# Four-row reads of the first part of each expert's down matrix, in a hybrid diffusion backbone on one Trainium2 core

## The chip, the core and the metric

The kernel runs on one core of one Trainium2 chip, in float32. A core has a matrix engine (PE, with its weight loads shown apart as PEld), a vector engine (DVE), a scalar engine (ACT), GpSimd (POOL), a synchronisation engine (SP) that here issues nearly all reads from device memory, and 16 DMA engines that move the data. The metric is device time of one launch in microseconds (us), the median of the runs; less is better. One MiB is 1.0486 MB.

## The reference

Two layers work on 256 latent tokens and 256 context tokens of width 1024. The first layer (attention beside a convolution, then a dense SwiGLU) and the mixer of the second (a state-space scan in two directions) are the same in both kernels. The change touches the last stage, the second layer's mixture of experts:

```python
logits = (hf @ w_router).astype(jnp.float32)
top_v, top_i = lax.top_k(logits, TOP_K)              # 2 of 8 experts for each of 256 tokens
top_w = jax.nn.softmax(top_v, axis=-1)
...
for e in range(N_EXPERTS):                           # w1, w3: 1024 x 3584, w2: 3584 x 1024
    out = out + gates[:, e:e + 1].astype(hf.dtype) * swiglu(hf, w1[e], w3[e], w2[e])
```

`swiglu(h, w1, w3, w2)` is `(silu(h @ w1) * (h @ w3)) @ w2`. The three matrices of one expert are 42 MiB, those of all eight 336 MiB (352 MB), and each is read once.

## The kernel before

A tile framework takes the Python program, schedules it with a timing model of its own, and writes one fixed queue of instructions for each engine. Each queue is worked off in order: an instruction that waits for a semaphore holds up all that stand behind it on its engine.

**The expert stage.** Eight experts are worked one after the other; here they are called expert 0 to 7 in that order. Only the tokens of an expert are gathered, in groups of 32: `GROUPS = (3, 2, 3, 2, 3, 2, 3, 1)`, the larger counts in the places with three groups. The hidden width of 3584 is split in two parts by `SS`: part 0 has 2048 columns (four blocks of 512, one for each quarter of PE's columns), part 1 has 1536 (four of 384). An expert's reads, in the order of its units, are:

- `up(0)`: 8 reads of w1 and 8 of w3, 128 x 2048, 1 MiB each (8 KB for each of the 128 partitions);
- `up(1)`: 8 of w1 and 8 of w3, 128 x 1536, 0.75 MiB each (6 KB for each partition);
- `down(0)`: 8 reads of w2, 1 MiB each: 256 rows, two adjacent rows (8 KB) to a partition;
- `down(1)`: 4 reads of the same kind, and 2 of 1 MiB in which each partition gets two single rows of 4 KB.

`turn(s)` transposes the hidden activations so that they fit the rows of `down(s)`; the transposes take every second column, because a partition holds two adjacent rows. `gather(e + 1)` fetches the next expert's tokens between `up(1)` and `down(0)`; `scatter` of an expert runs inside the next one. `slot_map` reads one small tile (`prow`) for each expert.

**Reads and slots.** `run` walks over the pieces of all experts and loads up to `AHEAD = 20` pieces ahead of the one that PE multiplies. Every read takes the next slot of a ring of 21 slots of 8 KB for each partition (`rings`, filled from the pools `rawe`, `t8`, `rawp`, `hlp` and `rawm`). A read is issued on SP (line 148, in `load`) and can't be issued before PE has finished with the slot's last content. Each read also carries one of eight completion semaphores in turn (`DMAHW0` to `DMAHW7` below), and waits for the read eight before it: no more than eight are under way.

In PE's queue the up matmuls are on line 1533, the down matmuls on line 1598, the gather on line 1486, the transposes on line 1566, the scatter on line 1622.

Of the kernel before, what the change touches and what calls it, by code (L numbers as in the profile page):

```python
# [10 lines left out]
F32 = mybir.dt.float32  # L11
# [8 lines left out]
P = 128  # L20
D = 1024
# [69 lines left out]
class Net:  # L91
# [44 lines left out]
    def load(self, view, pool=None):  # L136

        if isinstance(view, View):
            view = view.get()
        pieces = view if isinstance(view, list) else [(slice(0, P), view)]  # L140
        kk, n = pieces[0][1].shape[1:]
        if pool == "t8":
            t = self.wk([P, 2048], "t8")
        else:
            t = (pool or self.rawp).tile([P, 2048], F32, tag="hl" if pool is self.hlp else "raw", name=self.nm("raw"))
        v = t[:, :kk * n].rearrange("p (k n) -> p k n", k=kk)
        for sl, src in pieces:
            self.nc.sync.dma_start(v[sl], src)
        return v
# [17 lines left out]
    def run(self, units, ahead=2, pools=None):  # L167

        pieces = []
        for u in units:  # L170
            if u.views is None:
                pieces.append((u, None, 0, 0, 0, True, True))
                continue
            for vi, view in enumerate(u.views):
                kk, n = (view[0][1] if isinstance(view, list) else view).shape[1:]
                kp = max(1, self.SPLIT // n) if u.split else kk
                base = sum((w[0][1] if isinstance(w, list) else w).shape[1] for w in u.views[:vi])
                for k0 in range(0, kk, kp):
                    m = min(kp, kk - k0)
                    pieces.append((u, vi, k0, m, base, vi == 0 and k0 == 0,  # L180
                                   vi == len(u.views) - 1 and k0 + m == kk))
        loaded, parts, npc, seen, held = {}, {}, {}, {}, []
        for p in pieces:
            npc[id(p[0])] = npc.get(id(p[0]), 0) + 1
            seen[id(p[0])] = 0
        nxt = 0
        for i, (u, vi, k0, m, base, first, last) in enumerate(pieces):
            nahead = sum(1 for q in range(i + 1, nxt) if pieces[q][1] is not None)
            while nxt < len(pieces) and (nxt <= i or nahead < ahead):
                pu, pv, pk, pm, pb = pieces[nxt][:5]  # L190
                if pv is not None:
                    if (id(pu), pv) not in loaded:
                        loaded[id(pu), pv] = self.load(pu.views[pv], self.ring() if self.rings else None)
                    v = loaded[id(pu), pv]
                    sc = pu.scale(pb + pk) if pu.scale else None
                    parts[nxt] = self.wparts(v, pk, pm, sc) if pu.split else (v, None)
                    nahead += nxt > i
                nxt += 1
            if first and u.begin:
                u.begin()  # L200
            if vi is not None:
                hv, lv = parts.pop(i)
                if u.blocks and npc[id(u)] - seen[id(u)] <= u.tail:
                    held += [(base + k0 + c, hv[:, c], lv[:, c]) for c in range(m)]
                    for b in u.blocks if last else ():
                        for q in held:
                            u.mm(*q, [b])
                        u.end(b)
                else:
                    for c in range(m):  # L210
                        u.mm(base + k0 + c, hv[:, c], lv[:, c] if u.split else None)
                seen[id(u)] = seen.get(id(u), 0) + 1
            if last:
                held = []
                if u.end and not u.blocks:
                    u.end()
            self.tick()
# [1301 lines left out]
    def expert(self, e, n_g):  # L1519

        nc, A = self.nc, self.A
        st = {}
# [30 lines left out]
        def turn(s):  # L1553


            n = self.SS[s][1]

            def call():
                st["hT", s] = hT = self.wk([P, n // P, 3, P], f"hT{s}", bufs=1)
                for g in range(n_g):  # L1560
                    pt = self.ps("h")
                    for c in range(n // P):
                        t = st["g"][g][:, c // 2 * 256:c // 2 * 256 + min(256, n - c // 2 * 256)]
                        if t.shape[-1] == 256:
                            t = t.rearrange("p (i j) -> p j i", j=2)[:, c % 2]
                        nc.tensor.transpose(pt[:, c * P:(c + 1) * P], t, self.ident)
                    o, i = hT[:, :n // P, g], pt[:, :n].rearrange("p (c t) -> p c t", t=P)
                    if g % 2:
                        nc.vector.tensor_copy(o, i)
                    else:  # L1570
                        nc.scalar.copy(o, i)
            return Unit(begin=call)

        def down(s):
            r0, n = 4 * self.SS[s][0] // 4, self.SS[s][1]
            rows = lambda r, m: (lambda w: w[:, r:r + m])
            pair = lambda w: w.rearrange("o (i j) n -> i (o j) n", j=2)

            pieces = []
            for p in range(4):  # L1580
                for c in range(n // 256):
                    f = rows(r0 + n * p + 256 * c, 256)
                    pieces.append((lambda w, f=f: pair(f(w)), [(p, 2 * c), (p, 2 * c + 1)]))
            if n % 256:
                for p in (0, 2):
                    f = rows(r0 + n * p, 2 * n)
                    pieces.append((lambda w, f=f: f(w).rearrange("o (s i) n -> i (o s) n", s=2)[n - P:n],
                                   [(p, n // P - 1), (p + 1, n // P - 1)]))

            def begin():  # L1590
                if s == 0:
                    st["y"] = [self.ps("y") for _ in range(0, n_g, 2)]

            def mm(k, wv, _):
                p, c = pieces[k // 2][1][k % 2]
                for g in range(n_g):
                    for q in range(4):
                        nc.tensor.matmul(st["y"][g // 2][32 * q:32 * q + 32, g % 2 * 256:g % 2 * 256 + 256],  # L1598
                                         st["hT", s][:, c, g, 32 * p:32 * p + 32], wv[:, 256 * q:256 * q + 256],
                                         start=s == 0 and k == 0 and g % 2 == 0,  # L1600
                                         stop=s == 1 and k == 4 * n // P - 1 and (g % 2 == 1 or g == n_g - 1),
                                         tile_position=(0, 32 * q))

            return Unit([self.weights("od_ex_w2", e, [P, 2, D], f) for f, _ in pieces], mm, begin,
                        evict if s else None, False)

        def evict():
# [98 lines left out]
        self.n_ring += 1  # L1706
        return self.rings[self.n_ring % len(self.rings)]

    AHEAD = 20

    def late(self):

# [117 lines left out]
def build(tc, A, out, dbg=None):  # L1830
    net = Net(tc, A, out, dbg)
# [5 lines left out]
    with ExitStack() as ctx, tc.tile_pool(name="cp", bufs=1) as net.cp, \  # L1837
# [4 lines left out]
        with tc.tile_pool(name="t8p", bufs=9) as net.t8p, ExitStack() as early:  # L1842
            net.ecp = early.enter_context(tc.tile_pool(name="ecp", bufs=1))
            with tc.tile_pool(name="xcp", bufs=1) as net.xcp, tc.tile_pool(name="rawx", bufs=1) as net.rawx, \
                    tc.tile_pool(name="wp", bufs=1) as net.wp:
                with psum("psa", g=4, c=1, t=2, o=1) as net.psp:
                    h = net.phase1()
                with psum("psb", g=6, t=2) as net.psp:
                    h = net.phase1b(*h)
            with tc.tile_pool(name="op", bufs=1) as net.op, tc.tile_pool(name="wp2", bufs=1) as net.wp, \  # L1850
                    psum("psc", g=4, y=1, t=3) as net.psp:
                net.phase2(h)
            early.close()
            with psum("psm", h=6, y=2) as net.psp, tc.tile_pool(name="mp", bufs=1) as net.mp:
                net.t_tag = "h"
                with tc.tile_pool(name="rp", bufs=1) as net.wp:
                    net.route()
                with tc.tile_pool(name="ep", bufs=1) as net.wp, tc.tile_pool(name="rawm", bufs=5) as rawm:
                    net.rings = [net.rawe] + ["t8"] * 9 + [net.rawp] * 3 + [net.hlp] * 3 + [rawm] * 5
                    net.n_ring = -1  # L1860
                    net.moe()

# [12 lines left out]
```

## Time and profile before

| | us |
|---|---|
| median of 3 runs (1911.69 to 1915.6) | 1913.47 |
| the profiled execution's own time | 1911.85 |
| its span, first to last instruction | 1910.1 |
| expert stage, first up matmul to the end of the span | 1065.2 to 1910.1 |

How to read it: the page gives the busy share of each engine in 40 slices of the span, and what the DMA engines moved in each. A line of the timeline is a run of instructions of one kind on one engine, with the idle time just before it in brackets. A table of waits sums, for one engine, the time that it stood still, by what ended that wait. For SP a wait costs nothing by itself as long as earlier reads are still moving.

### The profile page before, as it was taken

Reading aid. Unit: us, or ns where it says so; the run is one execution under the profiler, and the core shown is the slowest. Engines: PE = TensorE matmul, PEld = TensorE weight load, DVE = VectorE, ACT = ScalarE, POOL = GpSimd, SP = SyncE. Lnnn points to the kernel's source line nnn. Section 1 sums busy time; section 2 is a strip of 40 time slices with the busy share of each in tenths; the row PEclk is TensorE's granted clock in tenths of the full one; section 3 lists DMA queues with packets and bytes.
Section 4 is the critical chain, followed back from the end, with each engine's and each line's share of the span. In section 5 each row is a group of like instructions: output and inputs, shape, how many; then the busy total and the mean of one; then the engine's idle time right before and its main releaser. Section 6 shows DMA issues by size and latency. Waiting matters only on the chain. (4 is left out here: it accounts for less than half of the span.)

```text
span 1910.1 us, 33591 instructions
## 1 busy us (share of the span) xinstructions
PE 1778.9 (93%) x14384; PEld 1110.9 (58%) x14384; DVE 703.5 (37%) x1143; ACT 519.1 (27%) x969; POOL 174.1 (9%) x167
## 2 busy tenths in 40 slices
PE   6999998999999989989989999999999999899964
PEld 3675356788888868757667445445644463435411
DVE  3395546334334356798887110101110101002001
ACT  3434454231222335756874100100000000001000
POOL 0064000000000014133320000000000000000000
PEclk8999999999999999989899899999999999999976
DMA  8543765422323243323357899999999999999995
GB/s 319 178 157 120 250 184 189 135 96 89 109 89 98 81 142 103 122 84 115 101 197 279 320 399 418 416 418 416 418 416 417 417 417 412 414 419 413 417 413 230
DMA packets 131574, 497.87 MB, mean 261 GB/s; under 512 B 11312, under 2 KB 18392, under 8 KB 102744
## 3 DMA queue, kind: packets, MB, share of 16 engines
q1 hardware_dynamic: 126808, 487.25, 66.3%
q10 hardware_dynamic: 4608, 8.39, 1.3%
q8 instruction: 115, 1.88, 0.4%
q14 instruction: 43, 0.35, 0.1%
HBM read 494.45 MB, written 1.15 MB: 259 GB/s over the span
## 5 line engine op out<-in xcount | busy, mean ns | idle before, releaser
L1533 PE MATMUL h<-raw,xe 128*32 128x512 f32 (+1 forms) x2664 | 265.6, 551 | 15.8 <-DMA raw<-in_od_ex_w_dram 15.8
L244 PE MATMUL g<-t,whl 128*128 128x512 f32 (+1 forms) x608 | 237.4, 390 | 0.0
L243 PE MATMUL g<-t,whl 128*128 128x512 f32 (+1 forms) x608 | 234.8, 396 | 2.1 <-ACT opad L1057 1.9
L245 PE MATMUL g<-t,whl 128*128 128x512 f32 (+1 forms) x608 | 232.7, 390 | 0.8 <-POOL whl L164 0.8
L1533 PE MATMUL h<-t,xe 128*32 128x384 f32 (+1 forms) x2200 | 214.9, 543 | 7.7 <-DMA t<-in_od_ex_w_dram 7.7
L164 DVE TENSOR_TENSOR whl<-raw,whl 128x1024 fp32r<-128x1024 f32 x109 | 137.7, 1266 | 206.6 <-ACT whl L161 206.1
L161 ACT CAST whl<-raw 128x1024 fp32r<-128x1024 f32 x129 | 134.5, 1049 | 269.9 <-PE g L245 234.3
L1533 PEld LDWEIGHTS h<-raw,xe 128*32 128x32 f32 x2664 | 97.8, 111 | 175.2 <-issue 113.2
L1544 DVE TENSOR_TENSOR g<-g,h 128x512 f32<-128x512 f32 (+1 forms) x38 | 23.6, 621 | 425.9 <-PE h L1533 238.6
L244 PE MATMUL g<-whl,t 128*128 128x512 f32 (+1 forms) x432 | 168.0, 392 | 9.2 <-DVE whl L164 7.3
L245 PE MATMUL g<-whl,t 128*128 128x512 f32 (+1 forms) x432 | 164.4, 389 | 0.0
L243 PE MATMUL g<-whl,t 128*128 128x512 f32 (+1 forms) x432 | 160.5, 394 | 1.9 <-DVE t L641 1.8
L1533 PEld LDWEIGHTS h<-t,xe 128*32 128x32 f32 x2200 | 79.1, 110 | 136.1 <-issue 91.8
L1598 PE MATMUL y<-raw,hT 128*32 128x256 f32 x2512 | 144.7, 388 | 9.7 <-DMA raw<-in_od_ex_w_dram 9.7
L1541 ACT ACTIVATE g<-h 128x512 f32<-128x512 f32 (+1 forms) x38 | 20.7, 544 | 448.9 <-PE h L1533 448.9
L243 PEld LDWEIGHTS g<-t,whl 128*128 128x128 f32 x608 | 116.6, 192 | 29.3 <-ACT opad L1057 2.3
L244 PEld LDWEIGHTS g<-t,whl 128*128 128x128 f32 x608 | 116.3, 191 | 23.7 <-issue 1.0
L245 PEld LDWEIGHTS g<-t,whl 128*128 128x128 f32 x608 | 115.4, 190 | 24.2 <-POOL whl L164 1.0
L428 POOL TENSOR_SCALAR rsv<-sst 128x1 f32<-128x1 f32 (+1 forms) x15 | 4.7, 311 | 1295.0 <-DVE sst L421 1294.8
L1598 PEld LDWEIGHTS y<-raw,hT 128*32 128x32 f32 x2512 | 80.0, 112 | 72.4 <-DMA raw<-in_od_ex_w_dram 15.0
L1598 PE MATMUL y<-t,hT 128*32 128x256 f32 x1744 | 103.4, 395 | 10.7 <-DMA t<-in_od_ex_w_dram 10.7
L1612 DVE TENSOR_TENSOR ys<-y,g2r 128x512 f32<-128x512 f32 (+1 forms) x12 | 6.6, 577 | 260.6 <-PE y L1598 260.6
(349 smaller groups left out, 2091.1 us busy)
## 6 DMA issues: line engine op xcount, KB each, us to landing
raw<-in_od_ex_w_dram SPq DMA_DIRECT2D x138, 1024.0 KB, 18.0
t<-in_od_ex_w_dram SPq DMA_DIRECT2D x102, 1024.0 KB, 19.2
raw<-in_od_ex_w_dram SPq DMA_DIRECT2D x68, 768.0 KB, 15.0
t<-in_od_ex_w_dram SPq DMA_DIRECT2D x60, 768.0 KB, 15.8
raw<-in_ev_ff_w_dram SPq DMA_DIRECT2D x32, 1024.0 KB, 5.1
raw<-in_ev_ada_w_dram SPq DMA_DIRECT2D x24, 1024.0 KB, 6.7
raw<-in_od_ada_w_dram SPq DMA_DIRECT2D x24, 1024.0 KB, 5.2
raw<-in_od_w_in_dram SPq DMA_DIRECT2D x20, 1024.0 KB, 5.2
```

Of the source, the lines that this page charges most:

```text
L161: self.nc.scalar.copy(hv, v[:, k0:k0 + m])
L164: eng.tensor_tensor(lv, v[:, k0:k0 + m], hv.bitcast(F32), op=ALU.subtract)
L243: mm(out, l[0], r[0], start=start, stop=False)
L244: mm(out, l[0], r[1], start=False, stop=False)
L245: mm(out, l[1], r[0], start=False, stop=stop)
L428: nc.gpsimd.tensor_scalar(v[:, :m], ss, inv_n, EPS, op0=ALU.mult, op1=ALU.add)
L1533: nc.tensor.matmul(st[i][g][32 * p:32 * p + 32, :n], st["x"][:, k, 32 * g:32 * g + 32], wv[:, n * p:n * p + n], start=k == 0, stop=k == KD ...
L1541: nc.scalar.activation(st["g"][g], st[0][g][:, :n], AF.Silu)
L1544: nc.vector.tensor_mul(st["g"][g], st["g"][g], st[1][g][:, :n])
L1598: nc.tensor.matmul(st["y"][g // 2][32 * q:32 * q + 32, g % 2 * 256:g % 2 * 256 + 256], st["hT", s][:, c, g, 32 * p:32 * p + 32], wv[:, 256 ...
L1612: nc.vector.tensor_tensor(ys[:, g:g + m], st["y"][g // 2][:, :256 * m].rearrange("p (g n) -> p g n", g=m), self.g2.unsqueeze(1).to_broadca ...
```

## The change

The first part of w2, 8 reads of 1 MiB for each expert, becomes 4 reads of 2 MiB: 512 rows, four adjacent rows (16 KB) to a partition. They go to a pool of their own, `rawb`, with two slots of 16 KB for each partition. Four slots of the small ring are given up for it, so that 17 are left, and `AHEAD` falls from 20 to 18. The transposes of part 0 take every fourth column instead of every second. Number and size of all matmuls stay as they are, and so do all other reads.

```diff
-        if pool == "t8":
+        if kk * n > 2048:
+            t = self.rawb.tile([P, 4096], F32, tag="rawb", name=self.nm("rawb"))
+        elif pool == "t8":
...
-                        loaded[id(pu), pv] = self.load(pu.views[pv], self.ring() if self.rings else None)
+                        big = isinstance(pu.views[pv], View) and np.prod(pu.views[pv].shape[1:]) > 2048
+                        loaded[id(pu), pv] = self.load(pu.views[pv], self.ring() if self.rings and not big else None)
...
-                        if t.shape[-1] == 256:
+                        if s == 0:
+                            t = st["g"][g].rearrange("p (i j) -> p j i", j=4)[:, c]
+                        elif t.shape[-1] == 256:
...
-                for c in range(n // 256):
+                for c in range(n // 256 if s else 0):
...
-            if n % 256:
+            if s == 0:
+                for p in range(4):
+                    f = rows(n * p, n)
+                    pieces.append((lambda w, f=f: f(w).rearrange("o (i j) n -> i (o j) n", j=4),
+                                   [(p, c) for c in range(4)]))
+            else:
...
-    AHEAD = 20
+    AHEAD = 18
...
-                with tc.tile_pool(name="ep", bufs=1) as net.wp, tc.tile_pool(name="rawm", bufs=5) as rawm:
-                    net.rings = [net.rawe] + ["t8"] * 9 + [net.rawp] * 3 + [net.hlp] * 3 + [rawm] * 5
+                with tc.tile_pool(name="ep", bufs=1) as net.wp, tc.tile_pool(name="rawm", bufs=1) as rawm, \
+                        tc.tile_pool(name="rawb", bufs=2) as net.rawb:
+                    net.rings = [net.rawe] + ["t8"] * 9 + [net.rawp] * 3 + [net.hlp] * 3 + [rawm]
```

The framework sets the queues anew for the changed program. All that stands ahead of the expert stage keeps its order. Two places of the expert stage, first SP's queue in expert 4 (three groups), where the reads of w2 begin. In these rows a name is that of the slot's tile, and the brackets hold the semaphores for which the instruction waits: `PE` is PE's, `DVE` that of DVE, `DMAHW`n those of reads. Before:

```order
L148 DMA t8_1693_11249<-in_od_ex_w3_dram 128x1536 [waits DMAHW5_49,PE_49]
...
L148 DMA t8_1694_11263<-in_od_ex_w2_dram 128x2048 [waits DMAHW6_49,PE_49]
...
L148 DMA t8_1695_11277<-in_od_ex_w2_dram 128x2048 [waits DMAHW7_49,PE_49]
...
L148 DMA raw_1706_11369<-in_od_ex_w2_dram 128x2048 [waits DMAHW2_49,PE_49]
L1501 DMA prow_1831_12732<-posd_1367_7901 128x2x128 [waits DMAHW3_49,DVE_49]
...
L148 DMA raw_1710_11386<-in_od_ex_w2_dram 128x2048 [waits DMAHW4_49,PE_49]
```

and now:

```order
L150 DMA raw_1677_11244<-in_od_ex_w3_dram 128x1536 [waits DMAHW5_49,PE_49]
...
L150 DMA rawb_1678_11258<-in_od_ex_w2_dram 128x4096 [waits DMAHW6_49]
...
L150 DMA rawb_1679_11272<-in_od_ex_w2_dram 128x4096 [waits DMAHW7_49]
L1504 DMA prow_1805_12683<-posd_1365_7900 128x2x128 [waits DMAHW0_49,DVE_49]
...
L150 DMA rawb_1688_11336<-in_od_ex_w2_dram 128x4096 [waits DMAHW6_49,DMAHW1_49,PE_49]
...
L150 DMA rawb_1692_11353<-in_od_ex_w2_dram 128x4096 [waits DMAHW7_49,DMAHW2_49,PE_49]
...
L150 DMA raw_1693_11367<-in_od_ex_w2_dram 128x2048 [waits DMAHW3_49]
```

The third big read (`rawb_1688`) takes the slot of the first, waits for PE to be done with it, and stands in SP's queue ahead of the six reads of `down(1)` and of all reads of expert 5. Experts 1 to 7 all have this order.

The second place is SP's queue around expert 0. There the first two big reads stand before the reads of `up(1)`, with no wait for PE:

```order
L150 DMA raw_1347_7771<-in_od_ex_w1_dram 128x1536 [waits DVE_49,DMAHW0_49,PE_49,Pool_49]
L150 DMA rawb_1376_8006<-in_od_ex_w2_dram 128x4096 [waits DMAHW1_49]
L150 DMA rawb_1377_8020<-in_od_ex_w2_dram 128x4096 [waits DMAHW2_49]
L150 DMA raw_1348_7773<-in_od_ex_w1_dram 128x1536 [waits DMAHW3_49,PE_49]
...
L150 DMA raw_1387_8087<-in_od_ex_w2_dram 128x2048 [waits DMAHW5_49,PE_49]
...
L150 DMA raw_1419_8453<-in_od_ex_w1_dram 128x2048 [waits DMAHW5_49,PE_49]
L150 DMA rawb_1382_8056<-in_od_ex_w2_dram 128x4096 [waits DMAHW6_49,PE_49]
L150 DMA rawb_1386_8073<-in_od_ex_w2_dram 128x4096 [waits DMAHW7_49,PE_49]
...
L150 DMA raw_1420_8503<-in_od_ex_w3_dram 128x2048 [waits DMAHW0_49,PE_49]
```

Before, these places held six reads of `up(1)` in a row, and the reads of `down(0)` followed those of `up(1)`:

```order
L148 DMA raw_1347_7768<-in_od_ex_w1_dram 128x1536 [waits DVE_49,DMAHW0_49,PE_49,Pool_49]
L148 DMA raw_1348_7770<-in_od_ex_w1_dram 128x1536 [waits DMAHW1_49]
L148 DMA raw_1349_7772<-in_od_ex_w1_dram 128x1536 [waits DMAHW2_49]
L148 DMA raw_1350_7774<-in_od_ex_w1_dram 128x1536 [waits DMAHW3_49]
L148 DMA raw_1351_7776<-in_od_ex_w1_dram 128x1536 [waits DMAHW4_49]
L148 DMA raw_1355_7793<-in_od_ex_w1_dram 128x1536 [waits DMAHW5_49,PE_49]
...
L148 DMA raw_1376_7979<-in_od_ex_w2_dram 128x2048 [waits DMAHW3_49,PE_49]
```

Now the third and fourth big read of expert 0 stand behind its six reads of `down(1)` and the first eleven reads of expert 1 (`raw_1419` is the eleventh). From `raw_1387`, the first read of `down(1)`, to `raw_1419` there are 17 small reads, so the next, `raw_1420`, takes the slot of `raw_1387`. PE's queue follows suit: four of expert 1's up pieces stand between the second and the third big piece of expert 0.

```order
L1608 MATMUL y_1417_8354<-rawb_1377_8020,hT0_1378_8037 32x256 x4
L1536 MATMUL h_1431_8720<-t8_1396_8187,xe_1408_8306 32x512 x4
...
L1536 MATMUL h_1432_8721<-t8_1402_8232,xe_1408_8306 32x512 x4
L1608 MATMUL y_1416_8353<-rawb_1382_8056,hT0_1378_8037 32x256 x8
...
L1608 MATMUL y_1416_8353<-raw_1387_8087,hT1_1411_8335 32x256 x8
```

Before, the pieces of expert 0's `down(0)` and `down(1)` stood there in a row, with none of expert 1 among them.

## Rows read from the trace of the kernel before

**Rows 1.** The page: the span in 40 slices, 47.75 us each.

```profile
PE   6999998999999989989989999999999999899964
PEclk8999999999999999989899899999999999999976
DMA  8543765422323243323357899999999999999995
GB/s 319 178 157 120 250 184 189 135 96 89 109 89 98 81 142 103 122 84 115 101 197 279 320 399 418 416 418 416 418 416 417 417 417 412 414 419 413 417 413 230
```

**Rows 2.** Stretches: us, busy us of each engine, granted clock, DMA share, GB/s.

```profile
core 0: us, PE busy (x) PEld busy (x) DVE busy (x) ACT busy (x) POOL busy (x), PEclk, DMA share, GB/s
1150.00:1200.00 50.00, 50.00 (x772) 24.94 (x768) 1.02 (x2) 1.19 (x2) 0.00 (x0) 1.00 1.01 417
1800.00:1850.00 50.00, 35.28 (x288) 8.55 (x280) 5.01 (x12) 1.67 (x3) 0.00 (x0) 0.83 1.01 413
...
1250.00:1284.00 34.00, 34.00 (x448) 14.38 (x444) 0.69 (x1) 1.05 (x2) 0.00 (x0) 1.00 1.01 419
1287.00:1312.00 25.00, 25.00 (x252) 10.34 (x248) 6.68 (x15) 1.17 (x2) 0.00 (x0) 1.00 1.01 416
```

**Rows 3.** What SP waited for, 1140 to 1890 us: total us, times, longest.

```profile
SPq L148 <- DMA raw<-in_od_ex_w_dram: 277.9, 157, 3.4
SPq L148 <- DMA t<-in_od_ex_w_dram: 205.7, 117, 3.3
SPq L148 <- PE y L1598: 35.7, 21, 6.9
SPq L148 <- PE h L1533: 27.1, 39, 1.3
```

**Rows 4.** Reads: count, KB each, median us from issue to landing; page, then 1023 to 1033 us.

```profile
raw<-in_od_ex_w_dram SPq DMA_DIRECT2D x138, 1024.0 KB, 18.0
...
t<-in_od_ex_w_dram SPq DMA_DIRECT2D x2, 1024.0 KB, 5.1
```

**Rows 5.** PE's timeline: expert 4 begins, its down part begins; the same of expert 6.

```profile
1465.84 1.06 PE L1533 MATMUL h<-raw,xe 128*32 128x512 f32 x8 [0.63 <-DMA raw<-in_od_ex_w_dram]
...
1547.21 7.11 PE L1598 MATMUL y<-t,hT 128*32 128x256 f32 x128
...
1680.72 3.64 PE L1533 MATMUL h<-t,xe 128*32 128x512 f32 x32 [0.64 <-DMA t<-in_od_ex_w_dram]
...
1762.52 7.86 PE L1598 MATMUL y<-raw,hT 128*32 128x256 f32 x120
```

**Rows 6.** PE's timeline: expert 0's down part, expert 1 begins, its down part begins.

```profile
1146.28 28.70 PE L1598 MATMUL y<-raw,hT 128*32 128x256 f32 x528
1174.80 7.95 PE L1598 MATMUL y<-t,hT 128*32 128x256 f32 x144
1182.57 7.91 PE L1533 MATMUL h<-t,xe 128*32 128x512 f32 x72
...
1239.35 12.29 PE L1598 MATMUL y<-raw,hT 128*32 128x256 f32 x224
```

**Rows 7.** PE's timeline: up and down pieces of expert 3; expert 5 from its last up piece.

```profile
1381.18 17.35 PE L1533 MATMUL h<-raw,xe 128*32 128x512 f32 x160
...
1437.97 14.02 PE L1598 MATMUL y<-t,hT 128*32 128x256 f32 x256
...
1641.50 1.50 PE L1533 MATMUL h<-t,xe 128*32 128x384 f32 x16 [0.38 <-DMA t<-in_od_ex_w_dram]
1642.93 3.81 PE L1486 MATMUL h<-pm,h 128*128 128x96 f32 x32
1646.58 0.87 PE L1566 MATMUL h<-ka,g 128*128 128x128 f32 x6
1647.38 3.00 PE L1598 MATMUL y<-raw,hT 128*32 128x256 f32 x50
```

**Rows 8.** PE's timeline: expert 7's last down piece, after the last read has landed.

```profile
1891.29 1.93 PE L1598 MATMUL y<-raw,hT 128*32 128x256 f32 x16 [1.45 <-DMA raw<-in_od_ex_w_dram]
```

More of the change, by code (lines that the diff above doesn't have):

```diff
@@ L1594, in mm @@
             def mm(k, wv, _):
-                p, c = pieces[k // 2][1][k % 2]
+                p, c = pieces[k // 2][1][k % 2] if s else pieces[k // 4][1][k % 4]
                 for g in range(n_g):
@@ L1602, in mm @@
                                          tile_position=(0, 32 * q))
-            return Unit([self.weights("od_ex_w2", e, [P, 2, D], f) for f, _ in pieces], mm, begin,
+            return Unit([self.weights("od_ex_w2", e, [P, len(a), D], f) for f, a in pieces], mm, begin,
                         evict if s else None, False)
```

## The prediction

> **What bounds the kernel now.** I began with the page's 40 slices. From slice 25 on (about 1150 us) the DMA engines are busy 9 tenths or more and move 412 to 419 GB/s to the end of the reads, while PE is also busy nearly all the time [rows 1]. The stretches tell the two apart: the DMA share is 1.01 there and the rate 416 to 419 GB/s whatever PE does, and in the last expert, where PE has 35 of 50 us of work, the rate is still 413 [rows 2]. So the reads set the end, and PE follows. PE is not far behind being a bound: with three groups it needs longer for an expert than the reads take, with two groups less. It falls behind in the even experts and catches up in the odd ones; in expert 4 and expert 6 it begins with the first read just landed (a wait for DMA ahead of the first piece), and by the last expert it waits for single reads [rows 5, 8].
>
> Then SP, which issues the reads. Its long waits are for earlier reads (483.6 us in 274 waits), not for PE (62.8 us) [rows 3]: eight reads are always under way, and a 1 MiB read lands 18.0 us after its issue, though a lone one takes 5.1 [rows 4]. Slots have not been what reads wait for. The question for the change is whether SP ever stands still so long that those eight run out, since idle time of the DMA engines is added to the end in full.
>
> **Prices.** From the first read of expert 4 to the first of expert 6, both waited for by PE, 84 MiB arrive in 1680.72 - 1465.84 = 214.9 us [rows 5]: 2.56 us for a MiB, 5.1 for a big read. A lone read takes 5.1 - 2.5 = 2.6 us beyond its transfer [rows 4]; I take that as the time from an issue into an empty queue to new data. PE's time for a big piece is 36.3 us / 672 x 96 matmuls = 5.2 us with three groups [rows 6], 14.02 / 256 x 64 = 3.5 with two [rows 7], and half of that, 1.75, with one.
>
> **What the change removes.** 64 reads become 32, and packets of 8 KB ones of 16 KB. Reads with 8 KB packets run at 419 GB/s, those with 6 KB at 416 [rows 2]. If a packet has a fixed cost, 0.7% between 6 and 8 KB makes 1.1% between 8 and 16: of 64 MiB x 2.51 = 161 us that is 1.7 us. From below it is bounded by nothing, from above by some 6 us (the same step three times over, as reading error of 419 and 416 allows). I take 2 us, near the row. The Trainium skill's HBM Reference, section Specifications, has a core streaming alone at about 425 GB/s; by that figure these reads could gain 2.3 us, as an estimate.
>
> Nothing else gets cheaper. The 76 transposes of part 0, at 0.87 / 6 = 0.145 us [rows 7], are 11 us in all; a stride of four for two would have to slow them by a third to cost 4 us, and that would fall on PE, which mostly follows. I cost it at nothing.
>
> **What the change adds: one wait per expert.** In experts 1 to 7 SP's queue now holds the third big read right behind the first two, and it waits until PE is done with the first. Behind it in SP's queue stand all further reads, so when the second big read has landed, the DMA engines have nothing left. Their idle time is: PE's end on the first big piece, plus 2.6, less the landing of the second.
>
> *Experts 2, 4, 6 (three groups).* Let time begin when PE starts on the first up read, just landed. PE reaches the first down piece 1547.21 - 1465.84 = 81.4 us later in expert 4, and 81.8 in expert 6 [rows 5]. By then 27 more MiB of up reads and the first big read have long landed: 29 x 2.56 = 74.2; the second at 79.3. PE ends the first big piece at 81.4 + 5.2 = 86.6, new data come at 89.2: idle 9.9 us. The fourth big read can be issued at 91.8, data at 94.4, when the third ends (94.3): 0.1. So 10 us each, 30 us for three. Expert 2 begins without a lag now, for the reason given under expert 1.
>
> *Experts 3, 5 (two groups).* Here PE catches up: 56.8 us from first up to first down piece [rows 7] against 28 x 2.56 = 71.7. Count from the landing of the last up read: PE needs its piece, the gather and the transposes, 1647.38 - 1641.50 = 5.9 us [rows 7], then 3.5: 9.4, new data at 12.0; the second big read has landed at 10.2. Idle 1.8 each, 3.6 for two. In expert 7, with one group, PE ends the first big piece before the second lands by more than 2.6: nothing.
>
> *Expert 1.* PE comes out of expert 0 with a long lag, since 16 reads lay ready when it began. It ends the third and fourth big piece of expert 0 at about 1174 (next paragraph) and `down(1)`, six pieces at 2.6, at 1189.6. Four up pieces of expert 1 are done by then (6.9 us), so its down part begins 1239.35 - 1182.57 - 6.9 = 49.9 us later [rows 6], at 1239.5, and the first big piece ends at 1243.0: new data at 1245.6. The reads: five more MiB of `up(0)` at PE's pace, the last landing at about 1192.2, then 12 MiB of `up(1)` and two big reads, 16 x 2.56 = 41.0: 1233.2. Idle 12.4. After it PE finds data later than it could use them, so the lag is gone at expert 2.
>
> *Expert 0.* Its first two big reads are loaded early, its third and fourth stand behind 11 reads of expert 1. PE begins down at 1146.28 [rows 6], ends the two big pieces at 1151.5 and 1156.7; the fourth read is issued then and lands at 1156.7 + 2.6 + 5.1 = 1164.4 if the queue is clear. PE does four up pieces (to 1163.6), two big pieces (1174.0) and the first piece of `down(1)` (1176.6). Only that frees the slot for the next small read, the seventeenth behind it: data at 1179.2, idle 14.8. Before, the rate stood at 417 GB/s from 1150 to 1200 [rows 2], so nothing is given back here.
>
> **The sum.** 30 + 3.6 + 12.4 + 14.8 = 60.8, less 2: +59 us of DMA idle time, in a stage whose end is the reads' end. Behind the last read the tail stays (one piece of 1.93 us, scatter and norm [rows 8]). Everything ahead of the stage keeps its order. On the profiled execution's span of 1910.1 this gives 1969, and its own time lies 1.75 above the span and 1.62 below the median of 1913.47: **1972 us** against that median.
>
> **The rivals.** *PE is never late at the big reads* (the reads run slower than I count, or PE faster). Then the idle time is 5.2 + 2.6 - 5.1 = 2.7 in three experts, 1.0 in three, and expert 0's 14.8 stays: +26 less 2, some 1937 us. Against it speak 81.4 and 81.8 us against 74. Chance 0.05.
>
> *The reads under way cover the wait, and only the packets count.* Eight reads of lead are 18 us [rows 4], more than any of the stalls above. If SP's wait lay within that lead, the gain of 2 us would remain, up to 6: 1908 to 1911.5, faster by over 0.2% (3.8 us, about what a measurement of this kernel can tell) only near its upper end. It decides if other reads stand behind the second big one when SP stops; in the order there are none, save in expert 0. Chance 0.04.
>
> *A fixed cost is saved with each read.* If the 2.6 us of a lone read were paid in the stream as well, 32 fewer reads would save 83 us: 1830. At a DMA share of 1.01 [rows 2] there is no room for it. Chance 0.01. The Trainium skill's DMA: Bandwidth & Descriptors, section Anatomy of one DMA, states such a fixed part, about 2.0 us for a DMA (on the GpSimd path), and by it, as an estimate, 64 us would go; rows 4 agree on a lone read, the stream's 18.0 us at 2.5 us apart shows it overlapped.
>
> *PE's clock falls in the new gaps.* In the last expert PE has gaps ahead of every read and the granted clock is 0.83, a mix of the two levels of 1.2 and 2.4 GHz [rows 2]. If the waits for the third big read did the same to experts 2, 4 and 6, their 117 us would grow by a fifth, 23 us each, most of it on the path: about 2030. The new gaps are single ones of a few us in over 100 us of work, not one ahead of each read. Chance 0.03.
>
> **How the numbers follow.** My forecast has 0.87: 1972 with its own bounds. If new data need no 2.6 us, about 16 us go from the seven stalls; if the packets save 6, another 4: 1951. At 2.51 us for a MiB the lag grows: +6; at twice the start-up, +18: 1996. The range of 1947 to 1990 leaves the ends and the rivals out, about 2 in 10. Slower by over 0.2%: 0.87 + 0.05 + 0.03 = 0.95. Within 0.2%: most of the covered case, 0.03. Faster: the rest of it and the fixed cost, 0.02.
>
> **What would show it.** Right: the row of SP's waits for PE on the down line grows by tens of us; in the slices of the expert stage DMA falls below 9 once per expert, deepest in experts 0, 1, 2, 4 and 6, and hardly in 3, 5 and 7; PE waits for the third big read 2 to 4 us; in between the rate stays near 417, or 419 in the big reads. Wrong: no dip in DMA at the w2 reads; or dips of the same depth in all experts, which would mean that PE's lag is not what sets them; or a new wait of PE in the up part, which would mean that 17 slots are too few there.

## The result and the profile after

The changed kernel takes 1977.34 us (median of 4 runs, 1973.18 to 1978.33), the kernel before 1914.05 (4 runs): a ratio of 1.0339, 95% interval 1.0322 to 1.0355, slower. The forecast was 1972. The profiled execution has a span of 1975.9 us, 65.8 more than before. The expert stage begins where it began (first up matmul at 1065.71 instead of 1065.2) and is 910.2 us long instead of 844.9: all of the loss lies in it.

The page of the kernel after: PE, its granted clock, the DMA engines and GB/s, 40 slices of 49.4 us each.

```profile
PE   6999998999999989998898999899989999899874
...
PEclk8999999999999999989998999999999999899876
DMA  8534674433232333523369979897999979997996
GB/s 311 190 135 148 213 203 160 136 98 106 87 107 75 113 124 97 156 81 123 138 208 400 350 307 383 345 418 303 419 388 419 401 314 418 382 419 305 413 421 265
```

Where [rows 1] has nine tenths from about 1150 us on, there are now slices of 303 to 345 GB/s. In the slices between them that hold no stall the rate is 413 to 421, as before or a little above, so the reads are not slower while they run; they stop. What SP waited for, 1140 to 1950 us (total, times, longest):

```profile
SPq L150 <- DMA t<-in_od_ex_w_dram: 184.9, 106, 2.9
SPq L150 <- DMA raw<-in_od_ex_w_dram: 161.3, 94, 2.5
SPq L150 <- PE y L1608: 138.1, 21, 19.2
SPq L150 <- DMA rawb<-in_od_ex_w_dram: 118.2, 17, 15.7
SPq L150 <- PE h L1536: 13.6, 23, 1.4
```

Against [rows 3] the wait for PE on the down matmuls has grown from 35.7 to 138.1 us. Expert 4's four big pieces on PE's timeline (start, us, line, operation, idle time before it), and under it the issue of the third and fourth big read on SP's:

```profile
1585.32 10.57 PE L1608 MATMUL y<-rawb,hT 128*32 128x256 f32 x192
1598.81 6.66 PE L1608 MATMUL y<-rawb,hT 128*32 128x256 f32 x96 [2.92 <-DMA rawb<-in_od_ex_w_dram]
1606.16 5.39 PE L1608 MATMUL y<-rawb,hT 128*32 128x256 f32 x96 [0.69 <-DMA rawb<-in_od_ex_w_dram]
```

```profile
1590.76 5.51 SPq L150 DMA_DIRECT2D rawb<-in_od_ex_w_dram  x2
```

PE needs 10.57 us for two big pieces, so it is done with the first at 1590.6, and at 1590.76 SP issues the third big read. It lands 8.0 us later, and PE, which goes on at 1598.81, has waited 2.92 us for it. The stretches around the down parts show what the reads lost; they are those of expert 0 to expert 7 in order (us; busy us of PE, PEld, DVE, ACT, POOL; granted clock; DMA share; GB/s):

```profile
1160.00:1190.00 30.00, 30.00 (x524) 16.79 (x519) 1.02 (x2) 0.00 (x0) 0.00 (x0) 1.00 0.59 230
1230.00:1260.00 30.00, 24.83 (x366) 15.03 (x362) 3.50 (x9) 2.17 (x5) 0.00 (x0) 0.94 0.60 240
1350.00:1380.00 30.00, 27.28 (x421) 17.23 (x414) 3.77 (x10) 2.40 (x6) 0.00 (x0) 0.94 0.61 237
1470.00:1490.00 20.00, 14.86 (x224) 7.42 (x216) 0.00 (x0) 0.00 (x0) 0.00 (x0) 0.83 0.91 362
1575.00:1615.00 40.00, 36.38 (x565) 21.75 (x561) 3.95 (x10) 2.40 (x6) 0.00 (x0) 0.96 0.68 268
1700.00:1720.00 20.00, 15.48 (x244) 8.15 (x240) 0.00 (x0) 0.00 (x0) 0.00 (x0) 0.82 0.87 351
1810.00:1840.00 30.00, 26.21 (x401) 16.70 (x397) 3.10 (x8) 2.31 (x6) 0.00 (x0) 0.94 0.60 233
1925.00:1945.00 20.00, 10.96 (x116) 4.72 (x120) 0.00 (x0) 0.00 (x0) 0.00 (x0) 0.67 0.92 373
```

A stretch of length L at rate r has lost L x (1 - r / 419) us of transfer, with the 419 GB/s of [rows 2]:

| expert (groups) | 0 (3) | 1 (2) | 2 (3) | 3 (2) | 4 (3) | 5 (2) | 6 (3) | 7 (1) | sum |
|---|---|---|---|---|---|---|---|---|---|
| forecast, us | 14.8 | 12.4 | 10 | 1.8 | 10 | 1.8 | 10 | 0 | 60.8 |
| lost, us | 13.5 | 12.8 | 13.0 | 2.7 | 14.4 | 3.2 | 13.3 | 2.2 | 75.1 |

### The profile page after: what moved, and what is told of

The parts are those of the page before. It is cut to its first block, busy times and chain, and to the rows that moved or that the text cites. A ratio compares the mean times of both kernels' runs of the same rounds, so it can differ in the third digit from the quotient of the medians.

```text
span 1975.9 us, 33351 instructions
## 1 busy us (share of the span) xinstructions
PE 1807.2 (91%) x14384; PEld 1107.0 (56%) x14384; DVE 703.3 (36%) x1143; ACT 517.9 (26%) x969; POOL 173.3 (9%) x167
## 5 line engine op out<-in xcount | busy, mean ns | idle before, releaser
L1536 PE MATMUL h<-t,xe 128*32 128x512 f32 (+1 forms) x2568 | 260.5, 551 | 18.6 <-DMA t<-in_od_ex_w_dram 18.5
L1536 PE MATMUL h<-raw,xe 128*32 128x384 f32 (+1 forms) x2296 | 226.8, 544 | 10.9 <-DMA raw<-in_od_ex_w_dram 10.9
L1608 PE MATMUL y<-rawb,hT 128*32 128x256 f32 x2432 | 153.0, 414 | 39.2 <-DMA rawb<-in_od_ex_w_dram 39.2
L1536 PEld LDWEIGHTS h<-t,xe 128*32 128x32 f32 x2568 | 86.2, 110 | 173.1 <-issue 121.4
L1536 PEld LDWEIGHTS h<-raw,xe 128*32 128x32 f32 x2296 | 79.8, 110 | 145.1 <-issue 104.2
L1608 PEld LDWEIGHTS y<-rawb,hT 128*32 128x32 f32 x2432 | 82.4, 119 | 107.8 <-DMA rawb<-in_od_ex_w_dram 44.5
L246 PEld LDWEIGHTS g<-whl,t 128*128 128x128 f32 x432 | 81.6, 190 | 27.4 <-issue 4.3
```

Of the source, the lines that this page charges most:

```text
L246: mm(out, l[0], r[0], start=start, stop=False)
L1536: nc.tensor.matmul(st[i][g][32 * p:32 * p + 32, :n], st["x"][:, k, 32 * g:32 * g + 32], wv[:, n * p:n * p + n], start=k == 0, stop=k == KD ...
```

## The experiments

The theory: SP's queue is in order, the third big read waits there for PE to be done with the first, and nothing else is issued until then; how long the DMA engines stand still is set by how late PE is. The rivals: reads of 2 MiB or packets of 16 KB are slow themselves; 17 small slots are too few; scarce big slots cost wherever their wait stands. Each ratio below is against runs of the kernel before on the same chip, with its 95% interval.

**Size of the reads: two reads of 1 MiB into each big slot.**

```diff
-            self.nc.sync.dma_start(v[sl], src)
+            for k in range(0, kk, 2) if kk == 4 and n == D and self.rings and kk * n > 2048 else ():
+                self.nc.sync.dma_start(v[sl, k:k + 2], src[:, k:k + 2])
...
```

> The changed kernel with each big slot filled by two reads of 1 MiB with 8 KB packets, in place of one of 2 MiB with 16 KB. Slots, waits and the order are as in the changed kernel. My theory: the waits for PE stay, and only what the larger packets save is lost, 2 to 3 us (with the third big read's first half landing sooner, PE may wait 2 us less, which changes nothing for the reads): 1975 to 1982. If the size of the reads or of the packets were the cause of the loss, the time would fall back to about 1914 to 1920.

Measured: 1975.39 us, 1.0340 (1.0305 to 1.0375), as slow as the changed kernel. Slots and order are the same, and SP stands 100.3 us for PE ahead of these reads, while reads and packets are those of before: the size of the reads is not the cause. Whether larger packets save 2 to 3 us can't be told from this run: its interval is some 7 us to either side.

**The ring alone: the kernel before with 17 slots.**

```diff
-    AHEAD = 20
+    AHEAD = 16
...
-                with tc.tile_pool(name="ep", bufs=1) as net.wp, tc.tile_pool(name="rawm", bufs=5) as rawm:
-                    net.rings = [net.rawe] + ["t8"] * 9 + [net.rawp] * 3 + [net.hlp] * 3 + [rawm] * 5
+                with tc.tile_pool(name="ep", bufs=1) as net.wp, tc.tile_pool(name="rawm", bufs=1) as rawm:
+                    net.rings = [net.rawe] + ["t8"] * 9 + [net.rawp] * 3 + [net.hlp] * 3 + [rawm]
```

> The kernel before with four slots of the ring taken away (17 instead of 21, 16 pieces ahead) and no big reads. My theory: 17 slots of 1 MiB are still more than twice the eight reads under way; only where PE lags by most, around expert 0 and 1, can a read find no free slot: 3 to 12 us, 1917 to 1926. The rival that the smaller ring is the cause gives about 1975.

Measured: 1921.80 us, 1.0045 (1.0021 to 1.0069). Four slots fewer cost about 9 us (4 to 13), not 63. In the trace a part of it stands at the start of the stage, in its first 55 us:

```profile
1071.50:1126.50 55.00, 55.00 (x545) 19.84 (x547) 6.11 (x22) 5.24 (x9) 0.00 (x0) 1.00 0.83 287
```

The kernel before moves 320 GB/s in the same stretch of its stage (1065.2 to 1120.2). From 1150 to 1400 us both run at 417. That is 4 us of the loss; where the rest stands is open.

**Scarce slots without big reads.** The kernel before, with the eight 1 MiB reads of part 0 in a pool of four slots of their own.

```diff
+        if pool == "own":
+            t = self.rawb.tile([P, 2048], F32, tag="rawb", name=self.nm("rawb"))
...
+            for v in views if s == 0 else ():
+                v.own = True
...
+                with tc.tile_pool(name="ep", bufs=1) as net.wp, tc.tile_pool(name="rawm", bufs=1) as rawm, \
+                        tc.tile_pool(name="rawb", bufs=4) as net.rawb:
```

> The kernel before, its eight 1 MiB reads of the first part unchanged in size, but in four slots of their own, with 17 slots for all other reads: the same memory as two big slots, without a big read. The fifth read then waits until PE is done with the first piece. My theory: the idle time of the DMA engines is as in the changed kernel less half of a big piece of PE, 2.6 us with three groups, 1.75 with two: about 7 to 10 us in experts 1, 2, 4 and 6, next to nothing in 3, 5 and 7, and 10 to 15 us at expert 0 if its later reads stand as far back: 1943 to 1960. If the size of the reads is the cause, it takes about as long as before, 1914 to 1926.

Measured: 1963.78 us, 1.0285 (1.0254 to 1.0317), 4 us above the top of what was expected, with the same 21 slots in all as before. Its stretches in expert 2 and expert 4:

```profile
1350.00:1380.00 30.00, 30.00 (x501) 19.41 (x497) 3.95 (x10) 2.40 (x6) 0.00 (x0) 1.00 0.67 268
...
1575.00:1605.00 30.00, 30.00 (x497) 19.27 (x492) 3.95 (x10) 2.37 (x6) 0.00 (x0) 1.00 0.66 264
```

They lost 10.8 and 11.1 us, where the changed kernel lost 13.0 and 14.4: less by 2.2 and 3.3 where half a big piece, 2.6, was expected, but more than the 7 to 10 that were expected of the stall itself; expert 1 lost 13.2 (234 GB/s from 1230 to 1260). So the loss comes with slots of their own that PE frees late, and the big read only adds the second half of its piece. It also says that slots are the cause only in this place, since the ring of 17 alone costs 9.

**The order: the second part's six reads between the second and the third big read.** Big reads, two big slots and the ring of 17 stay.

```diff
-        def down(s):
+        def down(s, part=None):
...
+            if s == 0:
+                pieces = pieces[:2] if part == 0 else pieces[2:]
...
-                [turn(0), up(1, 0, "od_ex_w1"), up(1, 1, "od_ex_w3")], [turn(1), down(0), down(1)],
+                [turn(0), up(1, 0, "od_ex_w1"), up(1, 1, "od_ex_w3")], [turn(1), down(0, 0), down(1), down(0, 1)],
```

> All four big reads, two big slots and the ring of 17 stay as in the changed kernel; only the order differs: two big pieces, then the six pieces of the second part, then the other two big pieces. The third big read then stands 6 MiB (15 us of transfer at 2.56 us for a MiB) further back in SP's queue. My theory gives: PE has ended the first big piece by then or nearly so (the stalls were 10 to 13 us with three groups), so 1916 to 1925, with the last read 2 MiB instead of 1, about 2 us of it behind the last read. If the big reads, their packets or the scarce slots cost by themselves, the time stays at about 1975.

Measured: 1918.95 us, 1.0047 (1.0031 to 1.0063). In its trace, SP's wait for PE over 1140 to 1890 us:

```profile
SPq L150 <- PE y L1613: 95.9, 18, 14.2
```

Expert 4's four big pieces on PE's timeline, the issue of the third and fourth big read on SP's, and the stretch around them:

```profile
1550.27 10.57 PE L1613 MATMUL y<-rawb,hT 128*32 128x256 f32 x192
...
1576.20 10.54 PE L1613 MATMUL y<-rawb,hT 128*32 128x256 f32 x192
```

```profile
1555.72 5.53 SPq L150 DMA_DIRECT2D rawb<-in_od_ex_w_dram  x2
```

```profile
1540.00:1600.00 60.00, 60.00 (x913) 32.97 (x908) 4.97 (x12) 2.71 (x7) 0.00 (x0) 1.00 1.00 409
```

The third big read again waits for PE and is issued when the first big piece is done, at 1555.72. SP still stands 95.9 us at such waits. But six reads were issued before it, the DMA engines work through them, and the rate stays at 409 GB/s with no gap on PE. This separates the wait from its price: it costs only when what was issued ahead of it runs out. What is left of the loss, 9 us, is as much as the ring of 17 costs alone, but it is not shown to be the same loss. It stands elsewhere, for the most part at expert 0 (8 us at the 418 GB/s that the kernel before has there):

```profile
1150.00:1190.00 40.00, 40.00 (x620) 19.83 (x612) 1.02 (x2) 0.85 (x2) 0.00 (x0) 1.00 0.85 335
```

Stalls of 2 to 3 us are left in experts 1, 2 and 6; in expert 6 SP waits 13.3 us for PE, and the rate is 303 GB/s from 1770 to 1780.

**Two of the four big reads only.** The other half of part 0 comes in 1 MiB reads through the ring; `AHEAD` is 19.

```diff
-                for p in range(4):
+                for p in range(2):
                     f = rows(n * p, n)
                     pieces.append((lambda w, f=f: f(w).rearrange("o (i j) n -> i (o j) n", j=4),
                                    [(p, c) for c in range(4)]))
+                for p in (2, 3):
+                    for h in range(2):
...
```

> Only the first two of each expert's four big reads stay; the other half of part 0 comes as four 1 MiB reads with 8 KB packets through the ring of 17. The two big slots are then used once per expert, so SP has no big read that waits for PE inside an expert. My theory (the loss is SP standing at the third big read until PE has done the first, while nothing else is queued ahead) gives: the wait of SP for PE on rawb is gone, and of +63 us only the cost of 17 small slots at expert 0 is left, some 5 to 8 us: 1917 to 1922. If the 2 MiB reads or their packets were slow themselves, half of them are still there and half of the loss stays: about 1945. If 17 small slots were what costs, the loss stays whole: about 1975.

Measured: 1914.62 us, 1.0015 (1.0002 to 1.0028), 3 us above before, a little less than expected, though the ring has 17 slots here too: what they cost depends on what else is loaded ahead. SP's wait for PE on the down line is back to what [rows 3] had (35.7):

```profile
SPq L150 <- PE y L1613: 36.0, 13, 17.0
```

**PE's lag taken away.** The same edit in both kernels: of the up matmuls of the second and third group only the first and the last step are kept.

```diff
-                for g in range(n_g):
+                for g in range(n_g if k in (0, KD - 1) else 1):
```

> The kernel before with most up matmuls of an expert's second and third group of 32 tokens left out (only the first and the last of the eight steps over the input width are kept), so that part of the up product is missing; all reads stay. PE then never falls behind. The reads set the end before, so my theory gives only the few us in which PE's pace counts around experts 0 and 1: 1900 to 1912. If PE were the bound, 1870 or less.

> The changed kernel with the same up matmuls left out (of the second and third group of 32 tokens only the first and the last of eight steps over the input width are kept, so part of the up product is missing). PE is then not late when the big reads come. My theory: the stall per expert shrinks to PE's piece plus 2.6 less 5.1 us, 2.7 with three groups and 1.0 with two, and expert 0's 12 to 15 us stay by the order: 20 to 28 us above the light kernel before, 1920 to 1938. If the cost lay in the reads, the slots or the packets and not in PE's lag, the difference would stay at 63 us, 1965 to 1975.

Measured: 1900.00 us, 0.9941 (0.9919 to 0.9964), and 1928.34, 1.0101 (1.0071 to 1.0131). The difference between the two is 28 us, where the full kernels differ by 63. In the light kernel with big reads, the stretches of expert 0, 2 and 4, and then PE's timeline in expert 4:

```profile
1155.00:1185.00 30.00, 29.32 (x496) 15.43 (x488) 2.40 (x4) 0.00 (x0) 0.00 (x0) 1.00 0.60 236
...
1330.00:1355.00 25.00, 21.55 (x376) 11.76 (x368) 0.00 (x0) 0.00 (x0) 0.00 (x0) 0.93 0.89 357
...
1550.00:1575.00 25.00, 22.36 (x388) 12.22 (x384) 0.00 (x0) 0.00 (x0) 0.00 (x0) 0.93 0.92 368
```

```profile
1545.63 10.57 PE L1608 MATMUL y<-rawb,hT 128*32 128x256 f32 x192
1558.83 12.05 PE L1608 MATMUL y<-rawb,hT 128*32 128x256 f32 x192 [2.63 <-DMA rawb<-in_od_ex_w_dram]
```

Experts 2 and 4 lose 3.7 and 3.0 us instead of 13.0 and 14.4, with the same down matmuls, big reads and slots. Only PE's arrival has changed, so its lag is the larger part of the stall there. Expert 0 still loses 13.1: its stall comes from the order of the queues. That the light kernel before is 12 us faster also shows that PE's pace counted for about that much before.

**SP's queue freed: the third and fourth big read issued on ACT.**

```diff
+        eng = self.nc.scalar if getattr(view, "act", False) else self.nc.sync
...
-            self.nc.sync.dma_start(v[sl], src)
+            eng.dma_start(v[sl], src)
...
+            for v in views[2:] if s == 0 else ():
+                v.act = True
...
```

> The third and fourth big read of each expert are issued from ACT's queue instead of SP's. Slots, sizes and the wait for PE are as in the changed kernel, but behind the waiting read SP's queue can go on: up to seven more reads until the completion semaphore of the third big read comes round, 7 x 2.56 = 18 us of transfer, against stalls of 10 to 13 us with three groups. My theory: the DMA engines keep moving in experts 1 to 6, PE waits longer for the third big read since it now shares the DMA engines with small reads, and most of the loss is gone: 1916 to 1935. If the scarce big slots cost by themselves, wherever the wait stands, or if large reads are slow, the time stays at about 1975.

Measured: 2001.17 us, 1.0480 (1.0447 to 1.0514): a miss, slower still. The framework set PE's queue anew with it. In expert 3 of this kernel PE's timeline, two stretches, and SP's wait for PE from 1497 to 1560 us:

```profile
1471.09 3.66 PE L1609 MATMUL y<-rawb,hT 128*32 128x256 f32 x64 [0.27 <-DMA rawb<-in_od_ex_w_dram]
1489.86 6.85 PE L1537 MATMUL h<-raw,xe 128*32 128x512 f32 x48 [15.11 <-DMA raw<-in_od_ex_w_dram]
...
1527.32 7.12 PE L1609 MATMUL y<-rawb,hT 128*32 128x256 f32 x128
1534.23 10.57 PE L1609 MATMUL y<-raw,hT 128*32 128x256 f32 x192
```

```profile
1472.00:1497.00 25.00, 9.89 (x108) 3.59 (x104) 0.00 (x0) 0.00 (x0) 0.00 (x0) 0.73 1.00 414
1500.00:1550.00 50.00, 45.34 (x560) 21.48 (x556) 0.69 (x1) 1.80 (x3) 0.00 (x0) 0.93 0.70 286
```

```profile
SPq L151 <- PE y L1609: 38.0, 6, 32.1
```

With SP free the reads do keep moving after the second big piece, at 414 GB/s. But PE's queue has expert 4's up pieces next, whose reads come behind the six of `down(1)`: PE stands 15.11 us. And the `down(1)` pieces come after them, at 1534.23, so their six slots stay taken, the ring of 17 is used up, and SP waits 32.1 us for the first to come free. It is the order that the changed kernel has around expert 0 alone, now in experts 0 to 6. What a second issuing queue would give with PE's order unchanged was not tried; the run leaves that open.

**Expert 0's stall alone.** Only expert 0 reads its part 0 in eight small reads.

```diff
+                    if e:
+                        pieces.append((lambda w, f=f: f(w).rearrange("o (i j) n -> i (o j) n", j=4),
+                                       [(p, c) for c in range(4)]))
+                    for h in () if e else range(2):
...
```

> The changed kernel, but expert 0 alone reads its part 0 in eight reads of 1 MiB through the ring of 17; experts 1 to 7 keep their four big reads. In the changed kernel the reads stood still 12.2 us at expert 0 and 12.8 us at expert 1. If the stalls add up one by one, as the prediction summed them, expert 0's goes and leaves the few us that 17 slots cost there: 1964 to 1970. The rival: PE works without a break from expert 0 into expert 1 and sets when expert 1's first big slot comes free, so reads that come earlier at expert 0 only wait longer at expert 1: the stall at expert 1 grows to 20 us or more, and the time stays at 1973 to 1978.

Measured: 1979.80 us, 1.0364 (1.0334 to 1.0394). The rival was right that nothing is gained (the time lies 2 us above its range), and wrong about the place. Its stretches at expert 0 and expert 1, its first 34 us of the stage, and the stage up to the third big read's arrival in expert 1; under them the last two for the changed kernel, and the last for the kernel before:

```profile
1160.00:1190.00 30.00, 30.00 (x528) 16.99 (x524) 1.02 (x2) 0.00 (x0) 0.00 (x0) 1.00 1.01 418
1235.00:1265.00 30.00, 24.79 (x366) 15.06 (x362) 3.50 (x9) 2.17 (x5) 0.00 (x0) 0.94 0.58 232
...
1070.60:1105.00 34.40, 34.40 (x321) 11.14 (x324) 3.35 (x18) 4.08 (x7) 0.00 (x0) 1.00 0.77 239
...
1070.60:1255.40 184.80, 179.59 (x2231) 83.61 (x2230) 20.30 (x56) 14.07 (x28) 0.00 (x0) 1.00 0.88 344
```

```profile
1065.70:1100.00 34.30, 34.30 (x320) 11.12 (x323) 2.58 (x16) 4.07 (x7) 0.00 (x0) 1.00 0.91 335
...
1065.70:1250.50 184.80, 179.63 (x2235) 83.57 (x2234) 20.31 (x56) 14.04 (x28) 0.00 (x0) 1.00 0.85 336
```

```profile
1065.20:1250.00 184.80, 184.80 (x2303) 85.82 (x2306) 20.30 (x56) 14.03 (x28) 0.00 (x0) 0.99 0.97 388
```

Expert 0's stall is gone (418 GB/s), expert 1's has hardly grown (13.4 us for 12.8). Yet from the first up matmul to the third big read of expert 1 both kernels take 184.8 us, with PE busy for 179.6 of them, and the whole stage takes 910.7 against 910.2 us. PE sets this stretch, as it did before without a break: a stall of the reads at expert 0 is one of several places where the reads can wait for PE. Here they waited at the start instead, where the big slots lay empty and the ring of 17 was soon full: 239 GB/s for 335. What the change costs in this stretch is the lead of the reads: 336 GB/s for 388 are 23 us of transfer. (That this kernel's stage begins 4.9 us later comes from ahead of the stage; why, no run settled. Over all profiled kernels here it begins between 1060.1 and 1072.1 us, so a few us of a total can come from there.)

## Why the prediction was right

**The mechanism** is shown: the kernel whose wait has nothing issued ahead of it loses 63 us, the one with six reads ahead of it 9 (the order moved), and the stalls of the three-group experts fall from 13 or 14 us to 3 or 4 when PE is not late (the light kernels). The signs named in advance are there: dips in experts 0, 1, 2, 4 and 6, hardly any in 3, 5 and 7, 413 to 421 GB/s between them, and SP's wait for PE up by 102 us. PE's wait for the third big read is 2.7 to 3.9 us in experts 2, 3, 4 and 6, as forecast, and 4.5 to 5.2 in 1, 5 and 7.

**Experts 2, 4 and 6** were put at 10 us and lost 13.0 to 14.4. In expert 4, from the first up piece at 1502.83: PE reaches the down part after 82.5 us (81.4 to 81.8 forecast), its piece takes 5.3 (5.2). The start-up was too short: the lone 2 MiB read takes 8.0 us, 3.1 beyond its 4.9 of transfer, not 2.6. And the price of a MiB was too high: in the trace of after, reads of 1 MiB land 2.48 to 2.49 us apart, not 2.56, so the second big read is there 77.7 us after the first up piece, not 79.3. With these numbers the prediction's own sum gives 13.2 us for the 9.9 of expert 4. Faster reads make a longer stall, since PE's lag grows by as much; the prediction gave this as +6 at 2.51 us.

**Experts 3 and 5** lost 2.7 and 3.2 for 1.8. The size is near, the path is not the one that was summed. PE was to be busy with gather and transposes when the first big read lands; it waited for that read, in expert 3 (first line) and expert 5:

```profile
1467.03 3.66 PE L1608 MATMUL y<-rawb,hT 128*32 128x256 f32 x64 [1.64 <-DMA rawb<-in_od_ex_w_dram]
...
1696.34 8.80 PE L1608 MATMUL y<-rawb,hT 128*32 128x256 f32 x128 [2.32 <-DMA rawb<-in_od_ex_w_dram]
```

So in expert 3 the stall is PE's piece, 3.66 us, and the start-up of 3.1, less the 4.9 us between the first and the second big read: 1.9 of the 2.7. In expert 5 the granted clock is 0.50 from 1698 to 1700, inside the first piece; the third big read is issued at 1701.75, 5.4 us after PE began, and the same sum gives 3.6 for the 3.2 lost. That the forecast of 1.8 lies near both is luck.

**Expert 1** lost 12.8 for 12.4, **expert 0** 13.5 for 14.8. But these were not two terms that stand apart: taking expert 0's away gave back nothing. The right reading of both is one stretch in which PE sets the time.

**Expert 7** was put at nothing and lost 2.2: the term was mis-sized. With one group PE waits for every read, and the granted clock is 0.67 in that stretch, a mix of 1.2 and 2.4 GHz. Its big pieces on PE's timeline:

```profile
1925.54 3.64 PE L1608 MATMUL y<-rawb,hT 128*32 128x256 f32 x32 [1.83 <-DMA rawb<-in_od_ex_w_dram]
1930.31 1.93 PE L1608 MATMUL y<-rawb,hT 128*32 128x256 f32 x32 [1.12 <-DMA rawb<-in_od_ex_w_dram]
1937.38 3.64 PE L1608 MATMUL y<-rawb,hT 128*32 128x256 f32 x32 [5.13 <-DMA rawb<-in_od_ex_w_dram]
```

The first piece takes 3.64 us after its wait, not 1.75, and the third big read is issued that much later. This is the clock rival, small, in the two experts (5 and 7) where it lengthens the stall. In expert 3 the clock falls only behind the issue of the third big read (0.57 from 1478 to 1482). In experts 2, 4 and 6 the granted clock around the stalls is 0.94 to 0.96, and only the piece behind the wait is longer (in expert 4, 6.66 us for 5.3).

**The sum.** 75.1 us were lost for 60.8 forecast, and the stage grew by 65.3 for 59: some 10 us came back that the prediction did not have. About 3 us came at the start of the stage, where the rate over the first 84.8 us is 368 GB/s for 354: the two big slots take 4 MiB early, where the four small ones given up for them held reads of 0.75 MiB. The rest is in the mean rate over the reads, before (first line, and its last 10 us under it) and after:

```profile
1120.00:1890.00 770.00, 727.44 (x9237) 350.96 (x9229) 73.77 (x171) 41.28 (x85) 0.00 (x0) 0.97 1.01 414
...
1880.00:1890.00 10.00, 7.58 (x72) 2.20 (x64) 0.00 (x0) 0.00 (x0) 0.00 (x0) 0.61 0.56 230
```

```profile
1120.00:1955.70 835.70, 755.40 (x9213) 347.83 (x9208) 73.03 (x171) 40.50 (x85) 0.00 (x0) 0.95 0.93 380
```

380 GB/s over 835.7 us are 417.5 over the 760.6 that are left without the stalls, against 414: worth 6.4 us. Less than half of it is a higher rate between the stalls, since before the rate is 416 up to 1870. Some 4.5 us lie in the last 10 us of the reads, where before it falls to 230; after, it is still 418 from 1945 to 1955.7 (more on this in the last section). So the 1972 stands 5 us from 1977 partly by luck: stalls that were put too short nearly cancel against a start and an end of the reads that got cheaper, which the prediction did not have.

**The packets**: the 2 us were not seen (1.0340 with packets of 8 KB, 1.0339 with 16 KB), and the runs are too coarse to show them. In the trace of after a packet of 16 KB took 613 ns and one of 8 KB 312 (medians): at most 2.8 us over the 256 large packets of each DMA engine. By the Trainium skill's HBM Reference, section Specifications, 2.3 us were to be had, as an estimate, at about 425 GB/s; the best slice here has 421, and no run shows that gain. **The transposes** with a stride of four cost what they cost before: in expert 1 the eight of part 0 take 1.23 us in both traces. (The 0.87 us for six in [rows 7], from which they were priced, are those of part 1, which did not change.) **The range**: 1947 lies below the 1951 of the prediction's own lower end, so it leaves out only the upper one.

**The other rivals.** That PE is never late is what the light kernels make true, and the loss is then 28 us, as the rival had it (24). That reads under way cover the wait is what happens in the kernel with the order moved, for most of its experts, and there alone. A fixed cost saved with each read was not seen anywhere: twice as many reads into the same slots took the same time.

## What to carry to other kernels

A queue that issues in order stops at its first wait, so the question for a new wait is how much is under way when it begins, against how late the engine is that must free the slot. Fewer, larger slots that are used twice in a row put that wait directly behind the last issue; the same slots with six other reads between the two uses lost 9 us in all instead of 63. Stalls in a stretch that another engine paces are not to be added one by one: measure the stretch from end to end.

## What was not expected of the hardware

One read is done when the last of the 16 DMA engines has signalled: in expert 4 the first signal of the third big read comes at 1597.75, the last at 1598.76, and PE goes on at 1598.81. In the trace of before, first and last signal of one read lie 3.5 us apart at 1196 us, 7.0 at 1402, 11.9 at 1609 and 11.0 at 1879; the kernel with 17 slots and the light one before drift in the same way (up to 11.8 and 11.9). After, where the stream is interrupted once per expert, they stay 0.7 to 3.7 apart. So in an unbroken stream some engines fall behind the others, and a stall lets them catch up. The end of the reads shows what it costs: before, the last read's first signal comes at 1880.35 and its last at 1891.24, and in between the engines that are done stand idle, at 230 GB/s from 1880 to 1890. After, the last read's signals lie 2.0 us apart. That is some 4.5 of the 10 us that came back in the sum. The drift is also in the 2.56 us for a MiB: between the two reads from which it was taken the last signals lie 214.9 us apart, the first ones 212.9. No run took the drift away by itself, and which engine falls behind, and why, stays open.
